# First chunk of x as float32 rows and half of w by sets of 128 rows on the hardware queues, with a wait ahead of GpSimd's loads

## The chip, the cores and the metric

The kernel runs on one core of one Trainium2 chip. The metric is device microseconds of one execution. "Time before" is the median of three runs; the profile is of one further execution.

## What is computed

```python
B, S, D = (16, 2048, 1024)          # x: B x S x D, w: D x D, decay: D, float32
xw = x @ w
out[:, 0, :] = xw[:, 0, :]
for t in range(1, S):
    out[:, t, :] = decay[None, :] * out[:, t - 1, :] + xw[:, t, :]
```

A matrix product with w, then along the sequence a running sum in which every column has its own decay.

## The kernel before, in words

The rows of x are cut into 64 chunks of 512 (TL) and taken mostly in pairs. A chunk has to be turned so that the columns of x lie on the partitions: `xt` holds it as [128, M=4, 2, 512] in bf16, where the eight contraction steps are k = 2m + e. The weights lie in `wsb`, [128, k, n, ...] in bf16, eight output groups n of 128 columns; n of 0 to 3 is the first half of w, 4 to 7 the second. A slot multiplies one group n with a chunk or a pair, eight matmuls for each chunk, and the result in PSUM is scanned by VectorE (DVE), or by ScalarE (ACT), GpSimd (POOL) and DVE together, turned back and stored.

In the steady part a chunk is loaded by GpSimd's software queue, which casts float32 to bf16 (`load`, line 101; four transfers, one for each quadrant of 32 partitions), turned in 32 x 32 blocks by DVE (`turn`, line 110) and copied into `xt` by ACT or DVE (`part`, line 119).

The opening is written out by hand. `pin` keeps every instruction in program order on its engine, and the string `agenda[-99]` is that order for the first 25 us: each word is a letter from the table `deeds` and a number. The letters that matter here:

- `U` (`load_part`): one quarter of w, a half h of the columns and a parity e of the rows, by four transfers of the software queue into `stage[h, e]`. U0 and U1 are the first half of the columns, U2 and U3 the second.
- `M` (`load_half`): half a chunk of x by the software queue. M1 is the second 256 rows of chunk 0, M2 and M3 are chunk 1. M0 isn't used: the first 256 rows come as float32 rows by the hardware queues of SyncE (SP) and ACT (lines 340 and 341).
- `H` and `J` (`gather`, line 374): DVE or ACT casts 128 of those rows to bf16 and puts the columns in order. `t` (`erect`, line 383): TensorE (PE) transposes them into PSUM with `eye`, which `I1` builds. `O` and `o` (`lay`, line 389): ACT or DVE copies them to `xt`.
- `E`, `F`, `G`: turn and copy for x that came through the software queue.
- `K` (`spin_on`, line 403): ACT copies a value of `stage[0, 0]` into a gate, and PE does two or three matmuls on it that nothing uses. Twelve more such matmuls open the program (line 354).
- `W` and `w` (`settle`, line 328): DVE or ACT moves one set of w (128 x 512) from `stage` to `wsb`; `q` and `Q` move one set in two pieces.
- `n` (`begin`, line 395): the matmuls of step 0 with even k, for the first 256 rows of chunk 0 (n0) and for the second (n1), 16 of 256 columns each. The odd k follow in step 0 (line 676), 16 of 512 columns, and then chunk 1 (lines 680 to 688). The second half of w is first used in step 4.
- `D` (`decays`, line 423): makes the decay columns from `rows`, which SP loads by four small transfers (line 356).

The staging areas lie in buffers that are free at the start: `room[0]` and `room[1]` are two output tiles.

Of the kernel before, what the change touches and what calls it, by code (L numbers as in the profile page):

```python
# [9 lines left out]
FP32 = mybir.dt.float32  # L10
BF16 = mybir.dt.bfloat16
# [3 lines left out]
def _ap(ap_obj: bass.AP, new_ap, extra_offset=0):  # L15
    return dataclasses.replace(
        ap_obj,
        ap=[list(p) for p in new_ap],
        offset=ap_obj.offset + extra_offset,
    )  # L20
# [5 lines left out]
def kernel(  # L26
# [26 lines left out]
    nc = tc.nc  # L53
    pin = tc.keep_in_program_order
    B, S, D = x.shape
    assert w.shape == (D, D)

    NQ = 4
    P = 32
    CQ = D // NQ  # L60
    K = CQ // P
    M = K // 2
    TL = 512
    NJ = TL // P
    NC = S // TL
    R = K // 2
    CH = D // 2
    CR = CH // NQ

    const = ctx.enter_context(tc.tile_pool(name="const", bufs=1))  # L70
    sb = ctx.enter_context(tc.tile_pool(name="sb", bufs=1))
# [4 lines left out]
    def ring(pool, name, count, shape, dtype=FP32):  # L76
        i = turns[name] = turns.get(name, -1) + 1
        return pool.tile(shape, dtype, name=f"{name}{i % count}")

    def quad(q):  # L80
        return slice(q * P, (q + 1) * P)
# [12 lines left out]
    def ot_tile(nj):  # L94
        return ring(sb, "ot", 4, [128, nj, CR])

    xb_of = {}
    xw_of = {}
    xt_of = {}
# [25 lines left out]
    def matmul(ps, n, k, xt, t0=0, t1=TL, start=0, pairs=None):  # L125
        if pairs is None:
            rhs = xt[:, k // 2, k % 2, t0:t1]
        else:
            rhs = pairs[:, k // 2, t0 // P:t1 // P, :, k % 2].rearrange("p j i -> p (j i)")
        lhs = wsb[:, k, n].rearrange("p q i -> p (q i)")  # L130
        pin(nc.tensor.matmul(  # L131
            out=ps[:, t0:t1] if ps.shape[1] >= t1 else ps,
            lhsT=lhs,
            rhs=rhs,
            start=(k == 0 and t0 == start),
            stop=(k == K - 1),
        ))
# [3 lines left out]
    class Tile:  # L141
# [39 lines left out]
        def copy(self):  # L181
            self.xs = sb.tile([128, 2 * TL], FP32, name=f"xs{self.lot % 3}")[:, 0:self.T]
            parts = self.ps if isinstance(self.ps, tuple) else (self.ps,)
            size = self.T // len(parts)
            for i, ps in enumerate(parts):
                pin(nc.scalar.copy(out=self.xs[:, i * size:(i + 1) * size], in_=ps))  # L186
# [103 lines left out]
    class Outlet:  # L290
# [8 lines left out]
        def store(self, b, t0, j0, j1):  # L299
# [4 lines left out]
            for j in range(j0, j1, nj):  # L304
# [8 lines left out]

    room = [ot_tile(2 * NJ).rearrange("p j c -> p (j c)") for _ in range(2)]
    size = M * CH
    stage = {(0, 0): room[0][:, 0:size // 2].bitcast(BF16),
             (0, 1): room[0][:, size:size * 3 // 2].bitcast(BF16),
             (1, 0): room[1][:, 0:size // 2].bitcast(BF16),
             (1, 1): room[1][:, size // 2:size].bitcast(BF16)}

    def load_w(queues, h, e):
        for i, q in enumerate((0, 2, 1, 3)):
            pin(queues[i % len(queues)].dma_start(  # L323
                out=stage[h, e][quad(q)].rearrange("p (m d) -> p m d", m=M),
                in_=_ap(w, [[2 * D, P], [2 * P * D, M], [1, CH]],
                        (q * CQ + e) * D + h * CH)))

    def settle(h, e, m, copy):
        src = stage[h, e][:, m * CH:(m + 1) * CH]
# [3 lines left out]
    idle = const.tile([128, TL], BF16, name="idle")  # L333
    spare = ring(psp, "spare", 1, [128, TL])
    rows = const.tile([128, 2, P], FP32, name="rows")
    touch = const.tile([128, 1], BF16, name="touch")
    H = NJ // 2
    halves = ((0, H), (H, NJ))
    whole = room[1][:, size:2 * size].rearrange("p (u c) -> p u c", u=2)
    for u, queue in enumerate((nc.sync, nc.scalar)):  # L340
        pin(queue.dma_start(out=whole[:, u], in_=_ap(x, [[D, 128], [1, D]], u * 128 * D)))
    pin(nc.vector.memset(idle, 0.0))  # L342
    pin(nc.vector.memset(rows, 0.0))
    pin(nc.scalar.copy(out=touch, in_=idle[:, 0:1]))

    gates = [const.tile([128, 128], BF16, name=f"gate{q}") for q in range(NQ)]
    for gate in gates:
        pin(nc.vector.memset(gate, 0.0))

    def spin(count, by):  # L350
        for _ in range(count):
            pin(nc.tensor.matmul(out=spare, lhsT=by, rhs=idle, start=True, stop=True))  # L352

    spin(12, idle[:, 0:128])
    for q in range(NQ):
        pin(nc.sync.dma_start(
            out=rows[q * P:q * P + R],
            in_=_ap(decay, [[P, R], [CH, 2], [1, P]], q * CR)))
    cols = const.tile([128, 2, P], FP32, name="cols")

    def load_half(i):
# [5 lines left out]
    firsts = [ps[:, 0:TL] for ps in heads] + [spares[0]]  # L367
    seconds = [ps[:, TL:2 * TL] for ps in heads] + [spares[1]]
    eye = const.tile([128, 128], BF16, name="eye")

    upright = room[0][:, size * 3 // 2:2 * size].bitcast(BF16).rearrange(
        "p (e u m c) -> p e u m c", e=2, u=2, m=M)

    def gather(i, copy):
        e, u = i // 2, i % 2
        pin(copy(out=upright[:, e, u].rearrange("p m (q i) -> p m q i", q=NQ),
                 in_=whole[:, u].rearrange(
                     "p (q m i e) -> p e m q i", q=NQ, m=M, e=2)[:, e]))

    def bed(e):  # L380
        return seconds[e].bitcast(BF16).rearrange("p (m t) -> p m t", m=M)

    def erect(i):
        e, u = i // 2, i % 2
        for m in range(M):
            pin(nc.tensor.transpose(
                out=bed(e)[:, m, u * 128:(u + 1) * 128], in_=upright[:, e, u, m], identity=eye))

    def lay(i, copy):
        e, m = i // 2, i % 2 * 2  # L390
        if 0 not in xt_of:
            xt_of[0] = ring(sb, "xt", 5, [128, M, 2, TL], BF16)
        pin(copy(out=xt_of[0][:, m:m + 2, e, 0:H * P], in_=bed(e)[:, m:m + 2]))

    def begin(i):
        for k in range(0, K, 2):
            for n in range(R):
                if i == 0:
                    matmul(firsts[n], n, k, xt_of[0], 0, H * P)
                else:  # L400
                    matmul(firsts[n], n, k, xt_of[0], H * P, TL, pairs=xw_of[0])

    def spin_on(q):
        pin(nc.scalar.copy(out=gates[q][quad(q), 0:1], in_=stage[0, 0][quad(q), 0:1]))
        spin(3 if q == 0 else 2, gates[q])

    def load_part(i):
        load_w((nc.gpsimd,), i // 2, i % 2)

    def part_one(i, copy):  # L410
        part(i // 8, copy, i % 4, i % 4 + 1, *halves[i // 4 % 2])
# [106 lines left out]
    def turn_and_load(c):  # L518
# [16 lines left out]
        "w": lambda i: settle_one(i, nc.scalar.copy),  # L535
        "M": load_half,
        "U": load_part,
        "E": lambda i: turn(i // 8, *halves[i // 4 % 2], i % 4, i % 4 + 1),
        "F": lambda i: part_one(i, nc.vector.tensor_copy),
        "G": lambda i: part_one(i, nc.scalar.copy),  # L540
        "K": spin_on,
        "t": erect,
        "H": lambda i: gather(i, nc.vector.tensor_copy),
        "J": lambda i: gather(i, nc.scalar.copy),
        "O": lambda i: lay(i, nc.scalar.copy),
        "o": lambda i: lay(i, nc.vector.tensor_copy),
        "n": begin,
        "q": lambda i: settle_slots(i, 0, 1),
        "Q": lambda i: settle_slots(i, 1, R),
# [19 lines left out]
        "L": lambda i: load(*loads.pop(0)) if loads else None,  # L569
    }  # L570
    agenda = {
# [92 lines left out]
    for step, (g, n) in enumerate(slots):  # L664
        T = TL * len(g)
        left = step - len(slots)
        if n % R == 0:
            ns, nj = range(n, n + R), T // P
            if left == -2 * R:
                outlets = [Outlet(ns, H, half) for half in range(2)]  # L670
            else:
# [4 lines left out]
        if step == 0:  # L676
# [3 lines left out]
            for k0 in range(0, K, 2):  # L680
                for i in range(R):
                    for k in (k0, k0 + 1):
                        matmul(seconds[i], i, k, xt_of[1], 0, H * P,
                               pairs=xw_of[1] if k0 < 4 else None)
            for i in range(R):
                for k in range(K):
                    matmul(seconds[i], i, k, xt_of[1], H * P, TL, H * P,
                           pairs=xw_of[1] if i < 2 else None)
        if step < R:
            ps = heads[n] if n < 3 else tuple(spares)  # L690
        else:
# [16 lines left out]
            elif step == K:  # L708
                todo = []
                nexts = (ring(psp, "spare", 1, [128, TL]), ring(psp, "ps", 3, [128, TL]))  # L710
                for l in range(len(g)):
                    for i, half in enumerate((ps[:, l * TL:(l + 1) * TL], nexts[l])):
                        for k in range(K):
                            matmul(half, n + i, k, xt_of.get(g[l]),
                                   pairs=xw_of[g[l]] if g[l] in (3,) else None)
# [51 lines left out]
```

## Time and profile before

| what | value |
|---|---|
| time, median of 3 runs | 903.61 us (903.51 to 903.97) |
| the profiled execution's own time | 903.72 us |
| its span | 901.9 us |
| PE busy | 891.2 us (99%) |
| DVE busy | 823.5 us (91%) |
| ACT busy | 687.1 us (76%) |
| POOL busy | 657.2 us (73%) |
| granted clock of PE | 1.0 |
| software queue q0 | 136,512 packets, 68.70 MB |
| SP's hardware queue q1 | 265,664 packets, 134.77 MB |
| ACT's hardware queue q10 | 144 packets, 0.52 MB |

A line of the timeline gives the start, the duration in us, the engine, the line of the kernel, the operation, what is written from what, the shapes and the count; in brackets stands how long the engine was idle before it and what ended that. PEld is the load of a stationary matrix. A line of the DMA answer gives a queue, its packets, the megabytes that it wrote and the time of its packets as a share of 16 engines over the stretch; packets of different queues overlap on an engine, so the shares can add up to more than 100%. A line of the windows gives a stretch in us, its length, then the busy times of PE, PEld, DVE, ACT and POOL, and then the granted clock, the DMA share and GB/s written.

### The profile page before, as it was taken

To read this page: it belongs to the slowest core of one execution; us is meant where nothing else is said; L and a number is where in the kernel's file an instruction comes from. 1 tells how busy PE (TensorE), PEld (TensorE's weight loads), DVE (VectorE), ACT (ScalarE), POOL (GpSimd) and SP (SyncE) were. 2 spreads that over 40 slices of the span, in tenths; PEclk is the share of its full clock that TensorE was granted. 3 is DMA by queue.
4 is the path that set the end of the run, shared out by engine and by line. 5 is a ranking of instruction groups with operands and counts; after the bars stand their busy time and mean duration, and the time that the engine had idled before them with its cause. 6 is when DMAs were issued, how large, how long until landed. Compare 5 with 4: busy or idle time off the path is not lost.

```text
span 901.9 us, 12229 instructions
## 1 busy us (share of the span) xinstructions
PE 891.2 (99%) x4131; PEld 411.9 (46%) x4213; DVE 823.5 (91%) x636; ACT 687.1 (76%) x962; POOL 657.2 (73%) x757
## 2 busy tenths in 40 slices
PE   8999999999999999999999999999999999999998
PEld 5544444444444444444444444444444444444444
DVE  4999998989999999999998999999999999999998
ACT  4889867778877877878778778777787787787743
POOL 8888678768767768677677687777777776876532
PEclk9999999999999999999999999999999999999999
DMA  9999999999999999999999999999999999999868
GB/s 193 195 215 218 229 212 207 216 233 247 247 248 255 248 255 252 246 254 250 222 235 228 218 236 227 233 226 227 232 230 227 227 236 222 226 228 221 177 153 231
DMA packets 402382, 204.77 MB, mean 227 GB/s; under 512 B 9360, under 2 KB 401552, under 8 KB 402320
## 3 DMA queue, kind: packets, MB, share of 16 engines
q1 hardware_dynamic: 265664, 134.77, 60.8%
q0 software_dynamic: 136512, 68.70, 56.8%
q8 instruction: 33, 0.54, 0.2%
q10 hardware_dynamic: 144, 0.52, 0.1%
q14 instruction: 29, 0.24, 0.1%
HBM read 138.42 MB, written 134.22 MB: 302 GB/s over the span
## 4 chain that ended last, share of the span: by engine, by line
PE 97%; DMA 1%; issue 1%; POOL 0%; DVE 0%; ACT 0%; DVEq 0%; POOLq 0%
PE ps L131 96%; PE spare L131 1%; DMA ot<-in_w_dram 1%; POOL ot L323 0%; DVE so L233 0%; PE ps L460 0%; PE spare L460 0%; ACT xb L467 0%; DVE wsb L419 0%; DVEq L419 0%; POOLq L751 0%
## 5 line engine op out<-in xcount | busy, mean ns | idle before, releaser
L131 PE MATMUL ps<-xt,wsb 128*128 128x512 bf16 (+1 forms) x3946 | 862.6, 378 | 4.7 <-DVE wsb L419 0.4
L131 PEld LDWEIGHTS <-wsb 128*128 128x128 bf16 x4160 | 406.5, 98 | 479.8 <-issue 0.9
L208 POOL TENSOR_TENSOR xs<-h,xs 128x512 f32<-128x512 f32 (+1 forms) x190 | 242.7, 1278 | 184.1 <-ACT h L169 83.1
L283 DVE STREAM_TRANSPOSE ot<-so 128x1024 f32<-128x1024 f32 (+2 forms) x265 | 300.2, 1171 | 6.5 <-DMA out_dram<-ot 4.4
L186 ACT COPY xs<-ps 128x1024 f32<-128x1024 f32 (+1 forms) x190 | 188.8, 994 | 149.3 <-PE ps L131 137.5
L266 POOL TENSOR_TENSOR so<-h,xs 128x512 f32<-128x512 f32 (+1 forms) x190 | 241.2, 1271 | 46.9 <-ACT h L169 27.2
L123 ACT COPY xt<-xw 128x2048 bf16<-128x2048 bf16 (+1 forms) x133 | 240.6, 1816 | 9.5 <-DVE xw L115 9.5
L105 POOL DMA_DIRECT2D xb<-in_x_dram x260 | 171.6, 661 | 2.9 <-DMA ot<-in_w_dram 0.9
L169 ACT ACTIVATE h<-so,dec 128x512 f32<-128x512 f32 (+1 forms) x190 | 145.3, 766 | 32.8 <-DVE so L213 29.9
L115 DVE STREAM_TRANSPOSE xw<-xb 128x2048 f32<-128x2048 f32 (+1 forms) x74 | 145.9, 1981 | 6.5 <-DMA xb<-in_x_dram 6.5
L213 DVE TENSOR_TENSOR_SCAN so<-spare,keep,xs 128x512 f32<-128x512 f32 (+1 forms) x97 | 119.8, 1237 | 25.9 <-POOL xs L208 25.6
L213 DVE TENSOR_TENSOR_SCAN so<-spare,xs 128x512 f32<-128x512 f32 x93 | 113.0, 1217 | 25.4 <-POOL xs L208 22.8
L169 ACT ACTIVATE h<-ps,dec 128x512 f32<-128x512 f32 (+1 forms) x189 | 129.3, 684 | 0.0
L233 DVE TENSOR_TENSOR_SCAN so<-dec,ps 128x1024 f32<-128x1024 f32 x34 | 76.9, 2260 | 0.8 <-ACT h L169 0.6
L233 DVE TENSOR_TENSOR_SCAN so<-dec,keep,ps 128x1024 f32<-128x1024 f32 (+2 forms) x35 | 74.7, 2138 | 0.0
L270 ACT COPY keep<-so 128x1 f32<-128x1 f32 x136 | 25.2, 188 | 9.1 <-DVE so L233 8.7
L204 ACT COPY so<-keep 128x1 f32<-128x1 f32 x97 | 18.4, 191 | 2.6 <-DVE ot L283 2.4
L131 PE MATMUL spare<-xt,wsb 128*128 128x512 bf16 (+1 forms) x68 | 14.0, 329 | 0.0
L323 POOL DMA_DIRECT2D ot<-in_w_dram x16 | 9.0, 561 | 2.9 <-POOLq L751 0.9
L202 POOL MEMSET so<- 128x1 f32 x93 | 10.7, 116 | 0.6 <-DVE ot L283 0.6
L131 PE MATMUL ps<-xw,wsb 128*128 128x256 bf16 (+1 forms) x56 | 9.3, 307 | 0.8 <-DVE xw L115 0.8
L352 PE MATMUL spare<-idle 128*128 128x512 bf16 x12 | 5.3, 632 | 1.2 <-DVE idle L342 1.2
(46 smaller groups left out, 43.9 us busy)
## 6 DMA issues: line engine op xcount, KB each, us to landing
out_dram<-ot SPq DMA_DIRECT2D x236, 512.0 KB, 10.8
xb<-in_x_dram POOLq DMA_DIRECT2D x248, 256.0 KB, 7.8
out_dram<-ot SPq DMA_DIRECT2D x56, 128.0 KB, 2.5
ot<-in_w_dram POOLq DMA_DIRECT2D x16, 128.0 KB, 5.6
out_dram<-ot SPq DMA_DIRECT2D x8, 256.0 KB, 4.2
xb<-in_x_dram POOLq DMA_DIRECT2D x12, 128.0 KB, 5.3
out_dram<-xb SPq DMA_DIRECT2D x4, 256.0 KB
ot<-in_x_dram ACTq DMA_DIRECT2D x1, 512.0 KB, 4.9
```

The costliest lines, as they stand in the source:

```text
L105: pin(nc.gpsimd.dma_start(out=xb_of[c][quad(q), j0:j1], in_=_ap(x, [[D, P], [P * D, j1 - j0], [1, CQ]], (b * S + t0 + j0 * P) * D + q * CQ)))
L115: pin(nc.vector.transpose(out=dst.rearrange("p (m j i) -> p j m i", m=M, i=P)[:, j0:j1, m0:m1], in_=src.rearrange("p (j m c) -> p j m c", ...
L123: pin(copy(out=xt_of[c][:, m0:m1, :, j0 * P:j1 * P], in_=src))
L131: pin(nc.tensor.matmul(out=ps[:, t0:t1] if ps.shape[1] >= t1 else ps, lhsT=lhs, rhs=rhs, start=(k == 0 and t0 == start), stop=(k == K - 1),))
L169: pin(nc.scalar.activation(out=h, in_=src, func=mybir.ActivationFunctionType.Copy, scale=dec[:, self.n:self.n + 1]))
L186: pin(nc.scalar.copy(out=self.xs[:, i * size:(i + 1) * size], in_=ps))
L208: pin(nc.gpsimd.tensor_tensor(out=odds, in0=self.g, in1=odds, op=ALU.add))
L213: pin(nc.vector.tensor_tensor_scan(out=so[:, 3:T + 2:2], data0=squares[-1][:, n:n + 1].to_broadcast([128, T // 2]), data1=self.xs[:, 1:T:2 ...
L233: pin(nc.vector.tensor_tensor_scan(out=so[:, t + 2:t + 2 + size], data0=dec[:, n:n + 1].to_broadcast([128, size]), data1=ps, initial=befor ...
L266: pin(nc.gpsimd.tensor_tensor(out=self.so[:, 2:T + 2:2], in0=self.h, in1=self.xs[:, 0:T:2], op=ALU.add))
L270: pin(nc.scalar.copy(out=self.keep, in_=self.so[:, self.T + 1:self.T + 2]))
L283: pin(nc.vector.transpose(out=outlet.ot[:, j:j + size, c0:c0 + P], in_=self.so[:, t1:t1 + size * P].rearrange("p (i t) -> p i t", t=P)))
```

## The change

The first 512 rows of x, not 256, come as float32 rows by the queues of SP and ACT, and are cast, transposed by PE and laid as the first 256 were. The second 256 rows lie until then in the buffer of chunk 0 that the software queue filled before (`xb_of[0]`), and the cast rows in `xw_of[0]`.

The first half of w also comes by the hardware queues, without a cast: `stage[0, e]` is float32 now, and `load_set` brings one set of 128 rows, 2 KB each, into 128 partitions, four for each e. SP's queue takes two transfers of x, then the sets (e, m) = (0, 0), (0, 2) and all four of e = 1, then the decay rows; ACT's takes two of x and the sets (0, 1) and (0, 3). U0, U1 and M1 are gone.

GpSimd first builds `eye`, then `hold` (`v`) copies two elements of `xt` that `o0` has written, and so waits for it; then come M2, M3, U2 and U3.

On PE, the gated matmuls become nine plain ones, then the transposes of the second 256 rows, one more plain one, and four matmuls of 512 columns for each even k (n0 to n3), each behind its own set of w. The order of the rest of the opening is as before.

```diff
-    stage = {(0, 0): room[0][:, 0:size // 2].bitcast(BF16),
-             (0, 1): room[0][:, size:size * 3 // 2].bitcast(BF16),
+    stage = {(0, 0): room[0][:, 0:size],
+             (0, 1): room[0][:, size:2 * size],
...
+    def load_rows(queue, i, u):
+        pin(queue.dma_start(
+            out=wholes[i][:, u], in_=_ap(x, [[D, 128], [1, D]], (2 * i + u) * 128 * D)))
+
+    def load_set(queue, e, m):
+        pin(queue.dma_start(
+            out=stage[0, e][:, m * CH:(m + 1) * CH],
+            in_=_ap(w, [[CQ * D, NQ], [2 * D, P], [1, CH]], (e + 2 * P * m) * D)))
+
+    load_rows(nc.sync, 0, 0)
+    load_rows(nc.scalar, 0, 1)
+    load_rows(nc.sync, 1, 0)
+    load_rows(nc.scalar, 1, 1)
+    load_set(nc.sync, 0, 0)
+    load_set(nc.scalar, 0, 1)
+    load_set(nc.sync, 0, 2)
+    load_set(nc.scalar, 0, 3)
+    for m in range(M):
+        load_set(nc.sync, 1, m)
...
-    gates = [const.tile([128, 128], BF16, name=f"gate{q}") for q in range(NQ)]
-    for gate in gates:
-        pin(nc.vector.memset(gate, 0.0))
...
-    def bed(e):
-        return seconds[e].bitcast(BF16).rearrange("p (m t) -> p m t", m=M)
+    def bed(h, e):
+        return seconds[2 * h + e].bitcast(BF16).rearrange("p (m t) -> p m t", m=M)
...
     def begin(i):
-        for k in range(0, K, 2):
-            for n in range(R):
-                if i == 0:
-                    matmul(firsts[n], n, k, xt_of[0], 0, H * P)
-                else:
-                    matmul(firsts[n], n, k, xt_of[0], H * P, TL, pairs=xw_of[0])
-
-    def spin_on(q):
-        pin(nc.scalar.copy(out=gates[q][quad(q), 0:1], in_=stage[0, 0][quad(q), 0:1]))
-        spin(3 if q == 0 else 2, gates[q])
+        for n in range(R):
+            matmul(firsts[n], n, 2 * i, xt_of[0])
+
+    def hold(i):
+        pin(nc.gpsimd.tensor_copy(out=held, in_=xt_of[0][:, 0, 0, 0:2]))
...
-        -99: "U0 I1 M1 U1 M2 M3 U2 U3 H0 J1 t0 t1 H2 J3 t2 t3 O1 o0 K0 O3 o2 K2 K1 K3 W0 W1 w2 W3 n0 E4 E5 G4 E6 G5 E7 F6 G7 n1 q4 w5 Q4 W6 W7 D E8 E9 G8 E10 G9 E11 F10 G11 E12 L E13 G12 L E14 G13 E15 L F14 G15",
+        -99: "I1 H0 J1 t0 t1 H2 J3 t2 t3 O1 o0 v M2 M3 U2 U3 O3 o2 K9 H4 J5 t4 t5 H6 J7 t6 t7 o4 O5 K1 W0 n0 o6 w1 n1 W2 O7 n2 W3 n3 q4 w5 Q4 W6 W7 D E8 E9 G8 E10 G9 E11 F10 G11 E12 L E13 G12 L E14 G13 E15 L F14 G15",
```

More of the change, by code (lines that the diff above doesn't have):

```diff
@@ L315, with load_w @@
     size = M * CH
-    stage = {(0, 0): room[0][:, 0:size // 2].bitcast(BF16),
-             (0, 1): room[0][:, size:size * 3 // 2].bitcast(BF16),
+    stage = {(0, 0): room[0][:, 0:size],
+             (0, 1): room[0][:, size:2 * size],
              (1, 0): room[1][:, 0:size // 2].bitcast(BF16),
              (1, 1): room[1][:, size // 2:size].bitcast(BF16)}
[L321 to L326, printed above, removed]
+    def load_w(queue, h, e, m0=0, m1=M, quads=range(NQ)):
+        for q in quads:
+            pin(queue.dma_start(
+                out=stage[h, e][quad(q), m0 * CH:m1 * CH].rearrange(
+                    "p (m d) -> p m d", d=CH),
+                in_=_ap(w, [[2 * D, P], [2 * P * D, m1 - m0], [1, CH]],
+                        (q * CQ + e + 2 * P * m0) * D + h * CH)))
     def settle(h, e, m, copy):
@@ L336 @@
     touch = const.tile([128, 1], BF16, name="touch")
+    held = const.tile([128, 2], BF16, name="held")
     H = NJ // 2
     halves = ((0, H), (H, NJ))
-    whole = room[1][:, size:2 * size].rearrange("p (u c) -> p u c", u=2)
-    for u, queue in enumerate((nc.sync, nc.scalar)):
-        pin(queue.dma_start(out=whole[:, u], in_=_ap(x, [[D, 128], [1, D]], u * 128 * D)))
+    xb_of[0] = ring(sb, "xb", 3, [128, NJ, CQ], BF16)
+    xw_of[0] = ring(sb, "xw", 2, [128, M, NJ, P, 2], BF16)
+    wholes = [room[1][:, size:2 * size],
+              xb_of[0].rearrange("p j c -> p (j c)").bitcast(FP32)]
+    wholes = [half.rearrange("p (u c) -> p u c", u=2) for half in wholes]
+    def load_rows(queue, i, u):
+        pin(queue.dma_start(
+            out=wholes[i][:, u], in_=_ap(x, [[D, 128], [1, D]], (2 * i + u) * 128 * D)))
+    def load_set(queue, e, m):
+        pin(queue.dma_start(
+            out=stage[0, e][:, m * CH:(m + 1) * CH],
[10 more added lines that the diff above has]
+        load_set(nc.sync, 1, m)
     pin(nc.vector.memset(idle, 0.0))
@@ L344, with spin @@
     pin(nc.scalar.copy(out=touch, in_=idle[:, 0:1]))
-    gates = [const.tile([128, 128], BF16, name=f"gate{q}") for q in range(NQ)]
-    for gate in gates:
-        pin(nc.vector.memset(gate, 0.0))
-    def spin(count, by):
+    def spin(count):
         for _ in range(count):
-            pin(nc.tensor.matmul(out=spare, lhsT=by, rhs=idle, start=True, stop=True))
-    spin(12, idle[:, 0:128])
+            pin(nc.tensor.matmul(
+                out=spare, lhsT=idle[:, 0:128], rhs=idle, start=True, stop=True))
+    spin(12)
     for q in range(NQ):
@@ L369 @@
     eye = const.tile([128, 128], BF16, name="eye")
-    upright = room[0][:, size * 3 // 2:2 * size].bitcast(BF16).rearrange(
-        "p (e u m c) -> p e u m c", e=2, u=2, m=M)
+    upright = xw_of[0].rearrange("p m j i e -> p (m j i e)").rearrange(
+        "p (h e u m c) -> p h e u m c", h=2, e=2, u=2, m=M)
     def gather(i, copy):
-        e, u = i // 2, i % 2
-        pin(copy(out=upright[:, e, u].rearrange("p m (q i) -> p m q i", q=NQ),
-                 in_=whole[:, u].rearrange(
+        h, e, u = i // 4, i // 2 % 2, i % 2
+        pin(copy(out=upright[:, h, e, u].rearrange("p m (q i) -> p m q i", q=NQ),
+                 in_=wholes[h][:, u].rearrange(
@@ L378, in gather @@
                      "p (q m i e) -> p e m q i", q=NQ, m=M, e=2)[:, e]))
-    def bed(e):
-        return seconds[e].bitcast(BF16).rearrange("p (m t) -> p m t", m=M)
+    def bed(h, e):
+        return seconds[2 * h + e].bitcast(BF16).rearrange("p (m t) -> p m t", m=M)
     def erect(i):
-        e, u = i // 2, i % 2
+        h, e, u = i // 4, i // 2 % 2, i % 2
         for m in range(M):
             pin(nc.tensor.transpose(
-                out=bed(e)[:, m, u * 128:(u + 1) * 128], in_=upright[:, e, u, m], identity=eye))
+                out=bed(h, e)[:, m, u * 128:(u + 1) * 128],
+                in_=upright[:, h, e, u, m], identity=eye))
@@ L389, in lay @@
     def lay(i, copy):
-        e, m = i // 2, i % 2 * 2
+        h, e, m = i // 4, i // 2 % 2, i % 2 * 2
         if 0 not in xt_of:
             xt_of[0] = ring(sb, "xt", 5, [128, M, 2, TL], BF16)
-        pin(copy(out=xt_of[0][:, m:m + 2, e, 0:H * P], in_=bed(e)[:, m:m + 2]))
+        pin(copy(out=xt_of[0][:, m:m + 2, e, h * H * P:(h + 1) * H * P],
+                 in_=bed(h, e)[:, m:m + 2]))
     def begin(i):
-        for k in range(0, K, 2):
-            for n in range(R):
-                if i == 0:
-                    matmul(firsts[n], n, k, xt_of[0], 0, H * P)
-                else:
-                    matmul(firsts[n], n, k, xt_of[0], H * P, TL, pairs=xw_of[0])
@@ L403, in spin_on @@
-    def spin_on(q):
-        pin(nc.scalar.copy(out=gates[q][quad(q), 0:1], in_=stage[0, 0][quad(q), 0:1]))
-        spin(3 if q == 0 else 2, gates[q])
+        for n in range(R):
+            matmul(firsts[n], n, 2 * i, xt_of[0])
+    def hold(i):
+        pin(nc.gpsimd.tensor_copy(out=held, in_=xt_of[0][:, 0, 0, 0:2]))
     def load_part(i):
-        load_w((nc.gpsimd,), i // 2, i % 2)
+        load_w(nc.gpsimd, i // 2, i % 2, quads=(0, 2, 1, 3))
     def part_one(i, copy):
@@ L540 @@
         "G": lambda i: part_one(i, nc.scalar.copy),
-        "K": spin_on,
+        "K": spin,
+        "v": hold,
         "t": erect,
```

## The prediction, made before the change was run

> **What bounds the kernel now.** I read the page's busy shares and chain of waits first, then the timeline of the first 30 us (the change touches nothing later), then the DMA answers for that stretch, last the windows with the DMA's rate. From the page:
>
> ```profile
> span 901.9 us, 12229 instructions
> PE 891.2 (99%) x4131; PEld 411.9 (46%) x4213; DVE 823.5 (91%) x636; ACT 687.1 (76%) x962; POOL 657.2 (73%) x757
> ...
> PE 97%; DMA 1%; issue 1%; POOL 0%; DVE 0%; ACT 0%; DVEq 0%; POOLq 0%
> ```
>
> TensorE carries 97% of the chain. Whatever delays its last gap moves the end by as much. The timeline shows where that gap is:
>
> ```profile
> 1.20 5.30 PE L352 MATMUL spare<-idle 128*128 128x512 bf16 x12 [1.20 <-DVE idle L342]
> ...
> 5.43 0.80 DVE L376 CAST ot<-ot 128x512 bf16<-128x512 f32 x2 [3.92 <-DMA ot<-in_x_dram]
> ...
> 6.29 1.34 PE L386 MATMUL ps<-eye,ot 128*128 128x128 bf16 x16
> ...
> 6.88 0.55 POOL L323 DMA_DIRECT2D ot<-in_w_dram  x1 [0.31 <-DMA ot<-in_w_dram]
> ...
> 9.86 1.31 POOL L105 DMA_DIRECT2D xb<-in_x_dram  x2
> ...
> 12.62 0.51 PE L131 MATMUL ps<-xw,wsb 128*128 128x256 bf16 x3 [0.76 <-DVE xw L115]
> ...
> 14.97 0.82 PE L131 MATMUL ps<-xt,wsb 128*128 128x512 bf16 x2 [0.37 <-DVE wsb L419]
> ...
> 18.43 0.84 PE L131 MATMUL ps<-xw,wsb 128*128 128x256 bf16 x6
> ```
>
> Sixteen even-k matmul pairs run from 9.95 to 14.6 with a gap of 0.76; after a gap of 0.37 the sixteen odd-k matmuls start at 14.97, when the second part of w has landed, and chunk 1 follows at 18.43. The waits show no idle TensorE after 14.97. So the measure is when the odd-k matmuls end: 18.43 now. One microsecond there is one at the end.
>
> **How the hardware queues cut a transfer.** This decides the case. The queue counts of the first 30 us:
>
> ```profile
> q1 hardware_dynamic: 192, 0.53, 5.9%
> q10 hardware_dynamic: 144, 0.52, 4.5%
> ```
>
> ScalarE's queue (q10) moved one transfer: 128 rows of x. 144 packets are 128 rows and 16 more. SyncE's queue (q1) moved the same (144) and the four decay transfers, so these took 48, 12 each: 8 pieces of 128 bytes and 4 more. The page's q1 total fits piece by piece: 236 x 1040 + 56 x 272 + 8 x 528 + 4 x 144 + 192 = 265,664, where every store (outer count 32 or 128) has 16 closing packets. I read the closing packets as one for each DMA engine used: transfers with an outer count of 32 or 128 run on 16 engines, those with 4 on 4.
>
> The new `load_set` has a source whose outermost count is NQ = 4 (then 32 rows, then 512 elements); its destination has 128 partitions. No row of before has unequal outer counts. The bounds are 16 engines (the 128 decides) and 4 (the 4 decides). I take 4: one cut must serve both sides, and with steps of 256 rows outside and 2 rows inside the source doesn't fold into 128. The decay transfers, whose source begins with the same count, are nearest.
>
> [...]
>
> **The change part by part.** Durations are those of the profiled execution (903.72 us, span 901.9), 0.11 above the median of 903.61.
>
> Removed: twelve GpSimd issues for the first half of w and x's second 256 rows (about 0.58 us each, 7 us), the gate copies and memsets, four DVE transposes (1.42) with their copies, and 32 matmuls of 256 columns (0.119 each, 3.8 us) for 16 of 512 (3.46): 0.35 saved, swallowed below.
>
> Rows of x: all 2.1 MB on two queues over 16 engines. The first megabyte allowed the casts at 5.43; bytes begin near 2.2, and the rate was:
>
> ```profile
> 3.00:4.00 1.00, 1.00 (x4) 0.33 (x3) 0.00 (x0) 0.00 (x0) 0.92 (x4) 1.00 1.05 430
> ...
> 899.00:900.00 1.00, 0.00 (x0) 0.00 (x0) 0.00 (x0) 0.00 (x0) 0.00 (x0) 1.00 1.06 389
> ```
>
> (Last columns: granted clock, DMA share, GB/s.) At 430 all of x is in by 2.2 + 4.9 = 7.1, call it 7.2. DVE is free for its casts at 8.82, when `o2` ends as now, so x costs nothing; its cover is lost if it comes after 9.1.
>
> TensorE's own order: transposes to 7.65, nine spins of 0.213 to 9.57, sixteen transposes (1.34) to 10.9, one spin to 11.1. DVE lays `o4` by 10.9 and casts `W0` by about 11.35 (0.44, priced by the casts of line 376: same shape and types). With w there, even k would run 11.35 to 14.8.
>
> Sets of w: 256 KB over 4 engines is 65.5 KB each. One engine's pace: 389/16 = 24.3 GB/s (one hardware queue with 2 KB rows, the stores at the end) up to 430/16 = 26.9. I take 24.3, the nearest in row size: 2.70 us a set, 21.6 for eight, one after another on the same four engines, since two queues share them. From 9.7 (first GpSimd issue 8.4, and 1.25 to movement as in the first issue now) software transfers want them too. What they take, from the first 5.5 us:
>
> ```profile
> q1 hardware_dynamic: 168, 0.53, 31.7%
> q10 hardware_dynamic: 144, 0.52, 24.5%
> q0 software_dynamic: 79, 0.08, 10.3%
> ```
>
> 10.3 of 66.5, that is 15%. So 2.5 us of the 21.6 are done by 9.7, and the other 19.1 take 19.1/0.845 = 22.6: the last set lands at 32.3. The first two land at 13.1, the next at 19.5, then one each 3.2. Bounds: 19.5 us with no software traffic, 26.7; all 4.2 MB of software traffic served first (10.8 on each engine), 39.6.
>
> Then `W7` (0.5) and four matmuls (0.87): odd k ends at 33.7 against 18.43, +15.3 (bounds +9.7, +22.6).
>
> Clock: the twelve opening spins start each 0.43 us, against 0.216 for the same form later, though the granted clock reads 1.00. If waiting brings that pace back, it costs between 0 and 2.35 (half of the 4.7 us that the opening lasted); no row decides, I take 1.2. [...]
>
> GpSimd's wait: behind `hold` queue M2, M3, U2, U3 and the `L` loads. It ends with `o0` near 8.3, and M2, issued at 9.86 now, starts at 8.4: free by itself. The ninth issue waits for the first landing (6.88 shows this limit), so U3 goes out only once M3 has landed, near 33, and lands by about 40; step 4 needs it after 41. Without that cover it would cost its lateness one for one.
>
> SyncE: the decay rows queue behind seven more transfers and land with the last set; `D` (0.57) and `E8` (0.36) follow `W7` in 0.95 while TensorE has 0.87: 0.1 or nothing. ScalarE issues three more (0.41 each, ended by 2.4), table load to 3.7, before its cast needs it at 5.
>
> Sum: 15.3 + 1.2 = 16.5; 903.72 + 16.5 = 920.2, or 920.1 on the median's scale. Own range: 913.3 (no software traffic, fast pace, no clock loss) to 928.6.
>
> **The rivals.**
>
> (a) The sets spread over 16 engines: not slower. Then 1 MB takes 2.5 us, even sets are in by 9.7 and odd ones, sharing with software traffic, by 13 to 15, when `W4` to `W7` want them at 14.5 to 17.1. Odd k starts at 14.8 instead of 14.97: 903.45. For it: stores from 32 partitions use 16. Against: the decay transfers' 4. It decides as soon as the odd sets land before 14.5.
>
> (b) As (a), but mixed traffic sinks to the slowest 2 us stretch of before, 158 GB/s written with the cast, 316 read: the 5.24 MB up to M2 need 16.6 us, 18.8 instead of 17.49, so chunk 1 waits 1.0 to 2.5: 905 to 906.
>
> (c) As (a), and faster by over 0.2%. TensorE's fixed order forbids even k before 11.1, so odd k before 14.57: a gain of 0.4 at most. It needs an effect that the trace doesn't show; 901.5.
>
> **How the numbers follow.** Measurement can tell about 0.2% (1.8 us) from no change. Chances: forecast 0.78, (a) 0.14, (b) 0.05, (c) 0.03. Predicted time 920. The range 905 to 928 takes in (b) and the forecast's bounds but for their last corner, and leaves out (a), (c). Slower 0.83, same 0.14, faster 0.03.
>
> **What would show it.** Right: TensorE waits on `wsb` copies near 13, 19 and then each three microseconds to about 32; DMA share far under 0.5 between 14 and 30 except where software queues fill it; 132 packets a set on the hardware queues. Wrong: 144 packets a set, odd k near 14.8, or a last landing outside 27 to 40. A wait on `xb` or `xt` ahead of `wsb` would upset the order of steps.

## The result, and the profile after

The changed kernel takes 930.87 us (median of 4 runs, 930.08 to 931.57) against 903.79 for the kernel before; the ratio is 1.0299, with a 95% interval of 1.0282 to 1.0317. It is 27.1 us slower. The prediction had the direction and the mechanism, but 920 in place of 931, and its range ended at 928.

The page of the changed kernel, whose profiled execution took 930.83 us:

```profile
span 929.0 us, 12296 instructions
PE 904.3 (97%) x4214; PEld 412.8 (44%) x4214; DVE 825.7 (89%) x631; ACT 687.2 (74%) x959; POOL 650.6 (70%) x746
...
PEclk7599999999999999999999999999999999999999
...
q1 hardware_dynamic: 266600, 136.86, 56.3%
q0 software_dynamic: 134272, 67.13, 55.0%
q10 hardware_dynamic: 552, 1.57, 0.5%
...
PE 95%; DMA 3%; SPq 1%; DVE 0%; issue 0%; ACT 0%
```

In the chain of waits DMA has risen from 1% to 3% of the span, and SyncE's queue (SPq) has come in with 1%. TensorE's granted clock is below 0.9 only in the first two of the 40 slices. The packets tell how the sets were cut: on ScalarE's queue 552 = 2 x 144 + 2 x 132, so a set of 128 rows closed with 4 packets, not 16 (ScalarE's queue carries two transfers of x and two sets). SyncE's count fits as well: 265,472 for the stores, 2 x 144 for x, 6 x 132 for sets and 48 for the decay rows are 266,600.

The timeline shows the sets arriving one by one and TensorE waiting for each:

```profile
9.65 1.19 ACT L397 CAST xw<-xb 128x512 bf16<-128x512 f32 x2 [1.59 <-DMA xb<-in_x_dram]
...
17.12 0.43 DVE L331 CAST wsb<-ot 128x512 bf16<-128x512 f32 x1 [5.91 <-DMA ot<-in_w_dram]
...
17.60 1.46 PE L131 MATMUL ps<-xt,wsb 128*128 128x512 bf16 x3 [6.10 <-DVE wsb L331]
...
23.73 0.87 DVE L331 CAST wsb<-ot 128x512 bf16<-128x512 f32 x2 [5.85 <-DMA ot<-in_w_dram]
...
28.34 0.49 DVE L437 CAST wsb<-ot 128x128 bf16<-128x128 f32 x2 [3.75 <-DMA ot<-in_w_dram]
...
32.46 0.62 ACT L331 CAST wsb<-ot 128x512 bf16<-128x512 f32 x1 [13.82 <-DMA ot<-in_w_dram]
...
36.80 0.43 DVE L331 CAST wsb<-ot 128x512 bf16<-128x512 f32 x1 [7.96 <-DMA ot<-in_w_dram]
...
41.96 0.43 DVE L331 CAST wsb<-ot 128x512 bf16<-128x512 f32 x1 [4.74 <-DMA ot<-in_w_dram]
...
43.01 0.24 DVE L442 STREAM_TRANSPOSE cols<-rows 128x64 f32<-128x64 f32 x1 [0.62 <-DMA rows<-in_decay_dram]
...
44.30 1.44 PE L131 MATMUL ps<-xw,wsb 128*128 128x256 bf16 x6
...
49.27 1.98 PE L131 MATMUL ps<-xw,wsb 128*128 128x256 bf16 x16
```

In the kernel before, chunk 1's first 32 matmuls end here:

```profile
21.99 1.98 PE L131 MATMUL ps<-xw,wsb 128*128 128x256 bf16 x16
```

The first cast of each set or pair of sets ends an idle time that the DMA caused. The sets weren't late because they were issued late: SyncE had issued its last one by 24.1 us, and four of the eight were cast between 28.34 and 41.96. Chunk 1 starts at 44.30 instead of 18.43: 25.9 of the 27.1. The rest is in chunk 1's first 32 matmuls, 44.30 to 49.27, 4.97 us instead of 3.56 (18.43 to 21.99), while the granted clock was at half until near 47.3 (0.50 from 44 to 47 us, 1.00 from 48); from these 27.3 the rest of the kernel takes back 0.2. Afterwards TensorE waits for nothing, as before.

The windows of the changed kernel (last columns: granted clock, DMA share, GB/s):

```profile
8.00:10.00 2.00, 1.63 (x11) 0.62 (x8) 1.27 (x4) 0.41 (x2) 1.91 (x4) 1.00 0.37 97
24.00:28.00 4.00, 3.19 (x8) 1.03 (x8) 0.58 (x2) 0.00 (x0) 1.08 (x2) 0.64 0.66 123
28.00:32.00 4.00, 1.09 (x4) 0.31 (x4) 0.49 (x2) 0.00 (x0) 0.90 (x2) 0.78 0.65 127
```

From 414 GB/s between 4 and 6 us the rate falls to 97 when the rows of x are nearly in. Between 8 and 9.5 us only the two hardware queues move, at 96 GB/s and a DMA share of 0.25. With the 4 closing packets I read that as four engines of sixteen, 24 GB/s for each, and twelve with nothing to do. (The 0.37 of the first row has the first software packets in it, from 9.6 us.) Later the rate is 123 to 127 with software traffic in it.

### The profile page after: what moved, and what is told of

Read it like the earlier page. It is cut to its first block, busy times and chain, and to the rows that moved or that the text cites. A ratio compares the mean times of both kernels' runs of the same rounds, so it can differ in the third digit from the quotient of the medians.

```text
span 929.0 us, 12296 instructions
## 1 busy us (share of the span) xinstructions
PE 904.3 (97%) x4214; PEld 412.8 (44%) x4214; DVE 825.7 (89%) x631; ACT 687.2 (74%) x959; POOL 650.6 (70%) x746
## 4 chain that ended last, share of the span: by engine, by line
PE 95%; DMA 3%; SPq 1%; DVE 0%; issue 0%; ACT 0%
PE ps L131 94%; DMA ot<-in_w_dram 2%; SPq L352 1%; PE spare L131 1%; DMA ot<-in_x_dram 1%; DVE so L233 0%; PE ps L478 0%; DVE wsb L331 0%; PE spare L478 0%; ACT xb L485 0%
## 5 line engine op out<-in xcount | busy, mean ns | idle before, releaser
L131 PE MATMUL ps<-xt,wsb 128*128 128x512 bf16 x4028 | 872.8, 379 | 19.3 <-DVE wsb L331 14.7
L105 POOL DMA_DIRECT2D xb<-in_x_dram x256 | 169.6, 663 | 4.6 <-DMA ot<-in_w_dram 3.2
L213 DVE TENSOR_TENSOR_SCAN so<-spare,keep,xs 128x512 f32<-128x512 f32 (+1 forms) x97 | 120.0, 1239 | 27.1 <-POOL xs L208 26.8
L331 DVE CAST wsb<-ot 128x512 bf16<-128x512 f32 x5 | 2.1, 427 | 24.5 <-DMA ot<-in_w_dram 24.5
L323 POOL DMA_DIRECT2D ot<-in_w_dram x8 | 4.3, 543 | 19.2 <-DMA xb<-in_x_dram 19.2
L131 PE MATMUL spare<-xt,wsb 128*128 128x512 bf16 (+1 forms) x68 | 16.0, 358 | 0.0
L331 ACT CAST wsb<-ot 128x512 bf16<-128x512 f32 x2 | 1.2, 618 | 19.5 <-DMA ot<-in_w_dram 19.5
```

The costliest lines, as they stand in the source:

```text
L105: pin(nc.gpsimd.dma_start(out=xb_of[c][quad(q), j0:j1], in_=_ap(x, [[D, P], [P * D, j1 - j0], [1, CQ]], (b * S + t0 + j0 * P) * D + q * CQ)))
L131: pin(nc.tensor.matmul(out=ps[:, t0:t1] if ps.shape[1] >= t1 else ps, lhsT=lhs, rhs=rhs, start=(k == 0 and t0 == start), stop=(k == K - 1),))
L213: pin(nc.vector.tensor_tensor_scan(out=so[:, 3:T + 2:2], data0=squares[-1][:, n:n + 1].to_broadcast([128, T // 2]), data1=self.xs[:, 1:T:2 ...
```

## The experiments

Two theories stood at first: the sets run on four engines, which they share with GpSimd's software transfers (A), or they are slow by themselves, as float32, by a late issue, or through the wait (B, C). Medians of the kernel before beside these runs were 903.74 to 903.96.

**e2_late_hold: no software transfer beside the sets.** GpSimd's wait is moved behind the cast of the last set.

```diff
-        pin(nc.gpsimd.tensor_copy(out=held, in_=xt_of[0][:, 0, 0, 0:2]))
+        pin(nc.gpsimd.tensor_copy(out=held, in_=wsb[:, 7, 0, 0, 0:2]))
```

In the agenda `o0 v M2 M3 U2 U3 O3` becomes `o0 O3`, and `W7 D` becomes `W7 v M2 M3 U2 U3 D`.

> As the change, but GpSimd waits until the last set of the first half of w has been cast, so that no software transfer runs beside the sets. Theory A, software transfers took turns with the sets on the same four engines: the odd sets land 2.7 us apart (65.5 KB at 24.3 GB/s), the last near 30 us, and the time is about 924 although chunk 1 comes late. Rival C, the sets are slow by themselves (a fixed cost or a late issue for each): they stay 4.2 us apart, the last near 40 us, and the time goes over 938.

Measured: 923.9 us in a single run, 7 us under the change although chunk 1 is asked for only at 30 us. Its windows, and the casts of DVE (ScalarE cast the set between 21.97 and 27.07 at 24.48):

```profile
20.00:24.00 4.00, 4.00 (x11) 1.46 (x12) 0.71 (x3) 0.00 (x0) 0.00 (x0) 0.55 0.26 102
```

```profile
14.34 0.43 DVE L331 CAST wsb<-ot 128x512 bf16<-128x512 f32 x1 [3.48 <-DMA ot<-in_w_dram]
...
21.97 0.50 DVE L437 CAST wsb<-ot 128x128 bf16<-128x128 f32 x2 [1.76 <-DMA ot<-in_w_dram]
27.07 0.43 DVE L331 CAST wsb<-ot 128x512 bf16<-128x512 f32 x1 [4.60 <-DMA ot<-in_w_dram]
29.61 0.43 DVE L331 CAST wsb<-ot 128x512 bf16<-128x512 f32 x1 [2.12 <-DMA ot<-in_w_dram]
```

The DMA share is 0.26, four of sixteen engines always busy, and 102 GB/s are 25.5 for each. The sets come 2.55 us apart ((29.61 - 21.97) / 3), in the change 4.54 ((41.96 - 28.34) / 3). If the four engines were as busy in the change as here (the trace has no row by engine), software traffic took 44% of their time (1 - 2.55 / 4.54). Theory C falls.

**e3_outer2: the first count of the source is 2.** Each set comes in two transfers of 64 rows.

```diff
-        pin(queue.dma_start(
-            out=stage[0, e][:, m * CH:(m + 1) * CH],
-            in_=_ap(w, [[CQ * D, NQ], [2 * D, P], [1, CH]], (e + 2 * P * m) * D)))
+        for q in (0, 2):
+            pin(queue.dma_start(
+                out=stage[0, e][q * P:(q + 2) * P, m * CH:(m + 1) * CH],
+                in_=_ap(w, [[CQ * D, 2], [2 * D, P], [1, CH]],
+                        (q * CQ + e + 2 * P * m) * D)))
```

> As the change, but each set comes in two transfers of 64 rows whose source begins with a count of 2. Theory A, the first count sets the number of engines: 66 packets a transfer (64 rows and 2), all on two engines, so that the sets take twice the time; the last lands near 60 us and the time is 945 to 955. Rival: the number of engines comes from something else (row size, steps of w in memory): the sets arrive as in the change and the time stays within 4 us of 930.9.

Measured: 958.27 us in a single run. ScalarE's queue again shows 552 packets, now 2 x 144 + 4 x 66: two closing packets a transfer. The last casts of DVE:

```profile
61.24 0.43 DVE L331 CAST wsb<-ot 128x512 bf16<-128x512 f32 x1 [18.85 <-DMA ot<-in_w_dram]
69.73 0.43 DVE L331 CAST wsb<-ot 128x512 bf16<-128x512 f32 x1 [8.06 <-DMA ot<-in_w_dram]
```

8.5 us between the last two sets, where the change has 5.2. From 10 to 16 us, before the first software packets, the sets moved at 51 GB/s, half of e2's 102. The first count of the source sets the number of engines here. My figure was again too low, by 3 to 13 us. At 25.5 GB/s two engines need 5.1 us for the 131 KB that each moves of a set (an estimate), so software traffic took about 40% here too; that its share was again taken too small fits, but no run of this form goes without software traffic to the last set.

**e1_quads: the same bytes on 16 engines.** Each transfer is a quadrant of 32 rows times four.

```diff
-    load_set(nc.sync, 0, 0)
-    load_set(nc.scalar, 0, 1)
-    load_set(nc.sync, 0, 2)
-    load_set(nc.scalar, 0, 3)
-    for m in range(M):
-        load_set(nc.sync, 1, m)
+    load_w(nc.sync, 0, 0, quads=(0,))
+    load_w(nc.scalar, 0, 0, quads=(1,))
+    load_w(nc.sync, 0, 0, quads=(2,))
+    load_w(nc.scalar, 0, 0, quads=(3,))
+    load_w(nc.sync, 0, 1)
```

> The same bytes of w by the same two hardware queues in the same number of transfers, but each transfer is one quadrant (source and destination begin with a count of 32) and not one set (source begins with 4). Theory A, four engines: 144 packets a transfer, the odd-k matmuls start between 14.5 and 15.5 us, time 903.5, within 902.8 to 905. Rival B, the loss comes from w as float32 on hardware queues or from GpSimd's wait, and not from the cut: time over 910, odd k after 20 us.

Measured: 907.65 us, ratio to before 1.0045 (1.0032 to 1.0058). 23 of the 27 us are gone, and ScalarE's queue has 576 = 4 x 144 packets. But neither figure of theory A came true: odd k starts at 20.20, which is one of the two signs that I had given rival B (its other, a time over 910, did not come). Two rows say where the time goes:

```profile
8.00:11.00 3.00, 2.31 (x23) 1.42 (x21) 1.55 (x4) 1.79 (x3) 3.00 (x6) 1.00 1.03 234
```

```profile
13.93 1.46 PE L131 MATMUL ps<-xt,wsb 128*128 128x512 bf16 x3 [3.62 <-DVE wsb L331]
```

All 16 engines are busy (1.03) and move 234 GB/s, not the 389 to 430 of the prediction's rows; the even sets are in at 13.4. And TensorE, idle for 3.6 us, runs its sixteen even-k matmuls in 6.27 us (13.93 to 20.20) instead of 3.46. The next two runs take these apart.

**e7_pairs: other quadrants at the same time.** As e1_quads, with SyncE filling quadrants 0 and 1 while ScalarE fills 2 and 3.

```diff
+    for q in (0, 1):
+        load_w(nc.sync, 0, 0, quads=(q,))
+        load_w(nc.scalar, 0, 0, quads=(q + 2,))
+    load_w(nc.sync, 0, 1, quads=(0, 1))
...
+        "s": lambda q: load_w(nc.scalar, 0, 1, quads=(q,)),
```

In the agenda `J7 t6` becomes `J7 s2 s3 t6`.

> As e1_quads, but the two queues fill quadrants 0 and 2, then 1 and 3, at the same time (0 and 1, then 2 and 3, and for the odd sets one queue alone before); ScalarE issues its two odd-set transfers after its last cast of x. Theory D, the 230 GB/s of e1_quads from 8 to 13 us came of which quadrants were filled together: the rate rises to 350 to 430, even k starts at 11.3 to 12, the clock holds, time 903.2 to 904.6. Rival: transfers of 32 partitions by hardware queues are slow by their shape: the rate stays near 230, even k starts near 13.9, time 907 to 908.5.

Measured: 907.02 us, ratio 1.0042 (1.0028 to 1.0056).

```profile
8.00:11.00 3.00, 2.18 (x22) 1.43 (x21) 1.55 (x4) 1.24 (x3) 2.96 (x6) 1.00 1.07 365
```

```profile
12.17 0.82 PE L131 MATMUL ps<-xt,wsb 128*128 128x512 bf16 x3 [1.99 <-DVE wsb L331]
...
18.23 0.87 PE L131 MATMUL ps<-xt,wsb 128*128 128x512 bf16 x3 [2.44 <-DVE wsb L435]
```

The rate is 365 GB/s with the same form of transfer, even k starts at 12.17 and the clock holds at 1.00: theory D as to the rate. The time lies in the rival's range (907 to 908.5), because odd k waited until 18.23 for its sets. ScalarE issued its last odd-set transfer only at 10.94 us, and that one moved between 15 and 18 us beside 0.42 MB of software traffic. I take the late issue for the cause, but it isn't shown: in e1_quads the odd sets were all issued by 9.6 us and were cast at 18.0 as well.

**e8_quads_warm: the clock.** As e1_quads, with `K14` for `K1` ahead of the even k.

> As e1_quads, with 14 matmuls that nothing uses, not one, in TensorE's gap before the even k. If the granted clock of 0.5 from 13 to 19.5 us is what made the sixteen even-k matmuls take 6.3 us instead of 3.5, it stays at 1.0 and the time is 2 to 3 us below e1_quads: 904.8 to 905.8. If the clock isn't on the path: within 0.7 of 907.65.

Measured: 906.92 us, ratio 1.0032 (1.0020 to 1.0045).

```profile
14.35 0.82 PE L131 MATMUL ps<-xt,wsb 128*128 128x512 bf16 x3 [0.67 <-DVE wsb L331]
...
18.67 0.82 PE L131 MATMUL ps<-xt,wsb 128*128 128x512 bf16 x3 [0.69 <-DVE wsb L436]
```

The granted clock stays at 1.00 from 13 to 19.5 us, where e1_quads has 0.50, and the even k take 14.35 to 17.81, 3.46 us in place of 6.27. That the low clock stretches these matmuls is shown. What it is worth in time is less than I expected: the odd sets are cast at 18.3 here and at 18.0 in e1_quads, so odd k starts at 18.67 after a wait of 0.7 (20.20 there). That is 1.5 us between the profiled executions (907.23 against 908.74, the slowest of e1_quads), but only 0.7 between the medians, just over the 0.7 that I had set for a clock that isn't on the path. My figure left out that the odd sets are next in line.

Of the 3.8 us that e1_quads is over the kernel before, e7 and e8 each take off less than one. No run removes both causes, so that they make up the whole isn't shown.

**e4_warm: the clock in the changed kernel.** Useless matmuls in the gaps, into a PSUM bank that is free there.

```diff
+    def warm(count):
+        for _ in range(count):
+            pin(nc.tensor.matmul(
+                out=seconds[0], lhsT=idle[:, 0:128], rhs=idle, start=True, stop=True))
...
+                if k > 1:
+                    warm(12)
                 for i in range(R):
                     matmul(firsts[i], i, k, xt_of[0])
```

In the agenda, with `r` for `warm`, `K1 W0` becomes `K1 r24 W0`, `n1 W2` becomes `n1 r17 W2` and `n3 q4` becomes `n3 r8 q4`.

> As the change, with TensorE kept busy in the gaps by matmuls that nothing uses (24, 17, 8 and three times 12). The sets should land as in the change. If the clock lost there is worth what the trace of the change shows (the last four odd-k matmuls 1.85 instead of 0.9 us, the first 32 matmuls of chunk 1 4.97 instead of 3.57), the time falls by 2.0 to 2.5 us. If the low clock costs nothing on the path, it stays within 0.7.

Measured: 930.63 us (928.6 to 932.0), so no gain that can be told in the median. Two of the four runs, 928.6 and 929.7, are faster than every run of the change, but the trace is of the slowest, and it says why the run does not decide the question. The last four odd-k matmuls are at full pace, but chunk 1 then waits for DVE, and the clock falls all the same after these short gaps (0.73 in 45 to 46 us, 0.50 in 46 to 48):

```profile
43.62 0.82 PE L131 MATMUL ps<-xt,wsb 128*128 128x512 bf16 x3 [1.74 <-DVE wsb L331]
...
45.31 1.34 PE L131 MATMUL ps<-xw,wsb 128*128 128x256 bf16 x6 [0.64 <-DVE xw L115]
```

**e5_x_only: the part on x alone.** The first half of w comes by the software queue, cast, ahead of the wait (`U0 I1 U1 H0 ...`, `stage[0, e]` in bf16 as before, no `load_set`).

> The part on x alone: 512 rows by the hardware queues and GpSimd's wait ahead of M2 to U3, but the first half of w by the software queue with its cast, as U0 and U1, ahead of that wait. Theory A: the loss goes with the sets of w; time 903.3 to 905, odd k between 14.6 and 16 us. Rival: the rows of x or the order of the opening carry part of the loss: over 907.

Measured: 903.98 us, ratio 1.0002 (0.9993 to 1.0011). Odd k starts at 15.33. The rows of x, the transposes, the order and the wait cost nothing that can be told.

**e6_quads_no_hold: the wait.** As e1_quads, with M2, M3, U2 and U3 issued right after `eye` and no `hold`.

> As e1_quads without GpSimd's wait: chunk 1 and the second half of w are issued from the first microsecond. Theory A: software traffic takes turns with the hardware queues from the start, the odd sets of w are in near 18 instead of 15 us, and the time is 2 to 4 us above e1_quads (905.5 to 907.5). Rival: the queues have room enough, and the wait is worth nothing: within 0.7 us of e1_quads.

Measured: 909.67 us, 2.0 above e1_quads; odd k starts at 20.63, held up by its sets (18.0 there, 20.34 here). The wait does good: it keeps software traffic off the sets. Between the profiled executions the difference is only 0.5 us (909.23 against 908.74), since that of e1_quads is its slowest.

## Why the prediction was right in kind and short in size

**Which number cuts a transfer: right.** "I take 4" rested on the decay transfers' 12 packets; the sets show 132 packets (128 and 4), e3 66 (64 and 2) and e1 144 (128 and 16). That one cut must serve both sides was an argument; the counts show only that the source's 4 decided against the destination's 128. That both queues use the same four engines, on which the 21.6 us rested, no row of before shows. The change does: from 8 to 9.5 us SyncE's queue had 12.2% and ScalarE's 13.2%, together the quarter that SyncE's queue alone had in e2 (26.3% from 20 to 24 us).

**The pace of one engine: right.** 24.3 GB/s taken, 25.5 measured alone (102 / 4). Without software traffic the sum gave a last landing of 28.8 (7.2 + 21.6); e2 has 29.6.

**The software share: the step that failed.** "10.3 of 66.5, that is 15%" made 3.5 us of it (32.3 - 28.8). It made 12.4 (41.96 against 29.61 in e2), and by the estimate above 44% of the time between the odd sets. The 15% came from 5.5 us in which the software queue had only begun to move: its first packets run at 4.8 us, 3.5 us after the first issue and not 1.25 as the prediction read it, and by 5.2 to 5.5 us, when the rows of x are in, its share is 123%. So the row was an average over a stretch in which the queue was mostly not there. (The start at 9.7 came true all the same, 9.6 in the change, by luck.) The row to take was a stretch in which the queue is loaded. In the kernel before that is:

```profile
28.00:30.00 2.00, 2.00 (x11) 0.86 (x10) 1.89 (x3) 1.12 (x6) 1.99 (x3) 1.00 1.45 196
```

Alone it writes 196 GB/s with the cast, 12.2 for each engine, so that M2 to U3 (2.1 MB written, 131 KB for each) need 10.8 us of any engine. That figure stood in the prediction as the far bound, 39.6 for the last landing. The change went 2.4 us past it: 0.8 of that is the later landing without software traffic, and from 37.3 us chunk 2's loads join in, beside which the last set took 5.2 us where the two before it took 4.1 and 4.3. How an engine divides its time among the queues no run shows; the 44% is an estimate of what it came to here.

**From the last set to chunk 1: 2.3 us, not 1.4.** Two things end together: the last four matmuls at half pace (42.45 to 44.30) and DVE, where the decay rows held `D` for 0.62 and `E8` ends near 44.2. "0.1 or nothing" for `D` and `E8` was too small; e4 shows that with the matmuls at full pace DVE's chain is what chunk 1 waits for (0.64 us there).

**The clock: 1.2 taken, 1.4 measured** on chunk 1's first 32 matmuls, which run without a gap. The 1.2 was picked between 0 and 2.35 with no row to decide it, so that it came near is luck. In the four odd-k matmuls before, its loss lay beside DVE's chain.

The sum with measured terms: last landing 41.96, 2.34 to chunk 1 and 1.41 of clock, less 18.43, is 27.3; the spans differ by 27.1. The prediction had 16.5. Of the 10.6 us missing, 8.9 are the software share, 0.8 the landing without it, 1.0 the step to chunk 1 and 0.2 the clock; 0.2 go the other way, after chunk 1 has begun.

**GpSimd's wait: as predicted, free** (e5), and better than free beside hardware transfers (e6). Its cover held in the change: U3's last transfer went out at 36.0 us, and the copies of the second half of w at 47.1 waited for no DMA. **The rows of x: nothing**, as predicted, though the last of them were cast at 9.65, as soon as they had landed, and not from 7.2 on. What held them up stays open: in e5, with no set on the hardware queues, it was 8.9. TensorE had slack until 17.

**Rival (a)** was tried only in a like form: e1 and e7 put w on 16 engines by quadrants and came to 907, not 903.45. Its "1 MB takes 2.5 us" (about 420 GB/s) did not hold: e1 moved 234 GB/s from 8 to 11 us, before any software packet, and e7 365. No version here beats the kernel before; e5 equals it.

## What to carry to other kernels

Before a transfer goes to a hardware queue, look at the first count of its source as well as its destination: with 4 there, 4 of 16 engines did all the work here, and the closing packets in the queue counts (132 for 128 rows) told it. Size a shared engine by what every queue will ask of it over the whole stretch, from a row where those queues are loaded, and not by the share of a queue that has only begun. A gap in TensorE's work can cost twice, once as the gap and once in the matmuls behind it: after 3.6 us of waiting in e1, sixteen matmuls took 6.27 us, and 3.46 in e8, where the gap was filled.

## What was not expected of the hardware

From 8 to 11 us, transfers of 32 partitions moved 234 GB/s where two queues filled neighbouring quadrants (first 0 and 1, in e1) and 365 where they filled quadrants 0 and 2 together, then 1 and 3 (e7), at a DMA share of 1.03 and 1.07. The engines were busy in both. The quadrants filled together and the rows of w read together both differ between the two, and no run separates them: where the limit was isn't shown.

In e4 the granted clock was 1.00 from 43 to 45 us, 0.73 from 45 to 46 and 0.50 from 46 to 48, after gaps of only 1.74 and 0.64 us with 1.0 us of matmuls between them (41.9 to 45.3 us).
